# Output projection of layer 1 by row blocks, with a new order of heads and every other weight unit of that mixer split on GpSimd

## The chip, the cores and the metric

The kernel runs on one core of one Trainium2 chip. The metric is the device time of one execution in microseconds (us). The engines are TensorE (PE, with PEld for its weight loads), VectorE (DVE), ScalarE (ACT), GpSimd (POOL) and SyncE (SP), which here issues nearly all DMAs.

## The reference

256 tokens of width 1024 go through two layers and a final RMSNorm, in float32. What the change touches lies in layer 1, between its two feed-forward halves (cut):

```python
u = rmsnorm(h, mix_norm[l])
proj = u @ b_w_q[j]                                  # 6 heads of 128 columns, then 256 for the memory queries
q = partial_rope(proj[..., :MIX_WIDTH]..., cos, sin)
q_mem = proj[..., MIX_WIDTH:]
lam = jnp.exp(jnp.sum(lp[0] * lp[1])) - jnp.exp(jnp.sum(lp[2] * lp[3])) + lam_init
o = differential_attention(q, k_sh, v_sh, lam)       # softmax 1 - lam * softmax 2, causal, times v
y_main = (rmsnorm(o, b_subln[j]) * (1.0 - lam_init)).reshape(b, s, MIX_WIDTH)
y_mem = memory_attention(q_mem, mk, mv)              # 4 heads over 256 memory rows
h = h + jnp.concatenate([y_main, y_mem], axis=-1) @ b_w_out[j]
h = h + 0.5 * swiglu(rmsnorm(h, ffn_post_norm[l]), ffn_post_w1[l], ffn_post_w2[l])
```

## The kernel before, in words

Activations lie transposed: 8 tiles of 128 features by 256 tokens. Every float32 weight comes by DMA into a "raw" tile (1 MB, `rawp`, 4 buffers) and is used in **units** of 128 x 1024 (`hlp`, 5 buffers). A unit is split in `emit_units`: ACT copies it to a reduced type (the high part `wh`, L187), DVE subtracts that from the raw weight (the low part `wl`, L188). Activations are split alike: high part on ACT (L262), low part on DVE (L263 or L268). A product is then three matmuls of 128 x 256 (`mm3`, L339 to L342) or two, of 256 and 512 columns (`mm_wide`, L344 to L348). `next_unit` (L194) hands out unit i and has units up to i+4 split ahead.

The mixer of layer 1 is a hand-written order, the string `ORDER_B` (L18), walked token by token in L903 to L932. With i the head or step: q = query projection of one unit (24 matmuls) and rope (shuffle L678 and product L679 on DVE, L680 and L681 on POOL); A = scores of a head, four maxima on DVE (L826), four exponentials on ACT (L832) and the combination of the two softmaxes on DVE (L834 to L837); T = its transposes on PE (L843) and the copy to SBUF on DVE (L845); P = product with the values on PE (L851 to L853), squares on ACT (L857) and the head's norm on DVE (L280 to L284, L860, L864); D = transposes back (L871) and the split of the result y (L262, L263). For the memory heads m = queries, S = scores (L575, maxima L581), t = transposes (L594) and copy (L596), p = product (L605), N = their norm, O = the way back.

G is a step of the output projection over the first four of its eight column blocks. `Group` (L392) takes four units of 128 output columns each and holds four PSUM tiles; G of step k adds what y[k] gives to each of the four (12 matmuls). After the loop `out_proj` (L488) adds these four blocks to the residual h and computes the other four with a whole unit each (16 matmuls by `mm_wide`). `done_into` (L498) splits each new block of h for the next feed-forward half and adds its square to an accumulator, on POOL for blocks 1 to 6. That half (`ffn_up`, L434) starts with two units of gate columns.

Each engine works through its own instructions in the order of the program; PE in particular doesn't step over a matmul whose operand is late.

Of the kernel before, what the change touches and what calls it, by code (L numbers as in the profile page):

```python
# [42 lines left out]
def decoder_trunk(  # L43
# [155 lines left out]

# [23 lines left out]
    for kp in (2, 3):  # L223
        load_x(2 * kp, 2)
        for o in (0, 1):
            load_w(kp, o, nc.sync)
    zero_b = const.tile([P, P], BF16, name="zero_b")
    V.memset(zero_b, 0.0)
    ps_w = psat.tile([P, 512], F32, tag="at", name="ps_w")
    for i in range(34):  # L230
# [11 lines left out]
    mask_b = const.tile([P, 3 * P], BF16, name="mask_b")  # L242
    V.memset(mask_b[:, P:2 * P], 0.0)
    for b in (0, 2):
        make_causal_mask(nc, mask_b[:, b * P:(b + 1) * P], mask_val=-1e30)
    pos_i = const.tile([P, T], I32, name="pos_i")
    rope_sb = const.tile([P, 2], F32, name="rope_sb")
    lam_sb = const.tile([P, 4 * HD], F32, name="lam_sb")

    def col(base, k):  # L250
        return cols_sb[:, base + k:base + k + 1]
# [140 lines left out]
    class Group:  # L392
        def __init__(self, n):
            self.ws = [next_unit() for _ in range(n)]
            self.ps = [mm_tile() for _ in range(n)]
            self.count = 0

        def run(self, u, ks):
            for w, ps in zip(self.ws, self.ps):
                for i, k in enumerate(ks):  # L400
                    n = self.count + i
                    mm3(ps, at(w, k), u[k], n == 0, n == KD - 1)
            self.count += len(ks)

    def proj_group(u, order=tuple(range(KD))):
        g = Group(2)
        g.run(u, order[:-1])
        g.run(u, order[-1:])
        return g.ps
# [15 lines left out]
    def first_blocks(u):  # L425
        pss = [wide_tile() for _ in range(4)]
        for kp in range(KD // 2):
            w = next_unit()
            for kk in range(2):
                k = 2 * kp + kk  # L430
                for i, ps in enumerate(pss):
                    mm_wide(ps, at(w, kk, slice(i * P, (i + 1) * P)), u[k], k == 0, k == KD - 1)
        return pss

    def ffn_up(u, nrm, after_first=None, rB=None, first=None):
# [49 lines left out]
            if d2 == 0 and after_first is not None:  # L485
                after_first()

    def out_proj(y, done, order, first=None):  # L488
        narrow = 0 if first is None else len(first)
        first = group_wide(y, order) if first is None else first  # L490
        for d in range(KD):
            ps = first[d] if d < len(first) else proj_wide(y, order)
            V.tensor_tensor(out=h[d], in0=ps[:, :T], in1=h[d], op=ALU.add)
            if d >= narrow:
                V.tensor_tensor(out=h[d], in0=ps[:, T:], in1=h[d], op=ALU.add)
            done(d)

    def done_into(nrm, gbase, eng=V):  # L498
# [61 lines left out]
    class MemAttn:  # L560
# [47 lines left out]
        def norm(self):  # L608
            rs = small.tile([P, 2, 4], F32, tag="mrs", name="mrs", bufs=1)
            V.reciprocal(rs, self.sm)  # L610
            on = tmp.tile([P, 2, 4, HD], F32, tag="eT", name="on")
# [16 lines left out]
    St = const.tile([P, T], F32, name="St")  # L628

    def rope_tables():  # L630
        ang = tmp.tile([P, T], F32, tag="t0", name="ang")
        V.tensor_copy(out=ang, in_=pos_i)
        V.tensor_scalar(out=ang, in0=ang, scalar1=rope_sb[:, 0:1], scalar2=None, op0=ALU.mult)
        est = tmp.tile([P, T], F32, tag="sd", name="est", bufs=1)
# [32 lines left out]
    shuf = [i + half if i < half else (i - half if i < ROT else i) for i in range(32)]  # L667

    def rope_scaled(rB):
        cr = tmp.tile([P, T], F32, tag="cr", name="cr", bufs=1)  # L670
        sr = tmp.tile([P, T], F32, tag="sr", name="sr", bufs=1)
# [57 lines left out]
    for j2 in range(3):  # L729
# [21 lines left out]
        step += 1  # L751
        for i in range(2):
            j = 2 * j2 + i
            bg = folded(proj_wide(u), "cr", bufs=1)
# [38 lines left out]
    lt = small.tile([P, 2, HD], F32, tag="lt", name="lt", bufs=1)
    lam4 = lam_sb.rearrange("p (a b d) -> p a b d", a=2, b=2)
    V.tensor_tensor(out=lt, in0=lam4[:, :, 0, :], in1=lam4[:, :, 1, :], op=ALU.mult)
    ls = small.tile([P, 2], F32, tag="ls", name="ls", bufs=1)
    V.tensor_reduce(out=ls, in_=lt, axis=AX.X, op=ALU.add)
# [105 lines left out]
    for tok in ORDER_B:  # L903
        c, i = tok[0], int(tok[1:] or 0)
        if c == "q":
            do_q(i, ready.pop(0) if tok in first else None)
        elif c == "m":
            qm[i] = mem_q(i, ready.pop(0) if tok in first else proj(u))
            if i == 1:
                ma = MemAttn(mkv1, qm, scol, True)  # L910
        elif c == "A":
            stage(i)
        elif c == "T":
            tr(i)
        elif c == "P":
            pv(i)
        elif c == "D":
            out_head(i)
        elif c == "S":
            ma.scores(i)  # L920
        elif c == "t":
            ma.tr(i)
        elif c == "p":
            ma.pv(i)
        elif c == "N":
            ma.norm()
# [117 lines left out]
```

## Time and profile before

| | |
|---|---|
| median of 3 runs | 980.94 us (980.48 to 982.2) |
| profiled execution: its time | 979.39 us |
| profiled execution: span in the trace | 977.6 us |
| PE busy | 961.7 us, 98% |
| DVE / ACT / POOL busy | 760.6 / 594.7 / 42.1 us |
| mixer of layer 1 on PE, first projection to the last output block | 706.07 to 784.51 us |

Busy time is the sum of an engine's instructions; a row of the timeline gives start, duration, engine, source line, operation, output and inputs, and in brackets how long the engine had stood idle before it and what ended that. PEclk is TensorE's granted clock, 1.00 for full speed. Durations of matmuls overlap, so the work of a group on PE is read from start to start.

### The profile page before, as it was taken

Reading aid. Unit: us, or ns where it says so; the run is one execution under the profiler, and the core shown is the slowest. Engines: PE = TensorE matmul, PEld = TensorE weight load, DVE = VectorE, ACT = ScalarE, POOL = GpSimd, SP = SyncE. Lnnn points to the kernel's source line nnn. Section 1 sums busy time; section 2 is a strip of 40 time slices with the busy share of each in tenths; the row PEclk is TensorE's granted clock in tenths of the full one; section 3 lists DMA queues with packets and bytes.
Section 4 is the critical chain, followed back from the end, with each engine's and each line's share of the span. In section 5 each row is a group of like instructions: output and inputs, shape, how many; then the busy total and the mean of one; then the engine's idle time right before and its main releaser. Section 6 shows DMA issues by size and latency. Waiting matters only on the chain.

```text
span 977.6 us, 15066 instructions
## 1 busy us (share of the span) xinstructions
PE 961.7 (98%) x5718; PEld 848.6 (87%) x5718; DVE 760.6 (78%) x1349; ACT 594.7 (61%) x1084; POOL 42.1 (4%) x55
## 2 busy tenths in 40 slices
PE   8999999999999999999999999999997999999997
PEld 7888888888888888888899888888896988888885
DVE  6977877697899987857797887867698688888553
ACT  6876665566556666655664666655558477666452
POOL 2000000001000000000050000000040100000000
PEclk9999999999999999999999999999998999999999
DMA  9866555554555656555556556466542256556441
GB/s 297 287 213 205 163 195 192 185 184 161 167 179 172 216 174 205 171 193 181 192 179 200 187 181 208 163 197 195 181 144 74 78 198 197 192 180 207 154 149 43
DMA packets 168968, 176.92 MB, mean 181 GB/s; under 512 B 3392, under 2 KB 163136, under 8 KB 168896
## 3 DMA queue, kind: packets, MB, share of 16 engines
q1 hardware_dynamic: 168320, 175.39, 55.3%
q8 instruction: 45, 0.74, 0.3%
q10 hardware_dynamic: 576, 0.57, 0.2%
q14 instruction: 27, 0.22, 0.1%
HBM read 174.90 MB, written 1.05 MB: 180 GB/s over the span
## 4 chain that ended last, share of the span: by engine, by line
PE 93%; DVE 4%; ACT 1%; issue 0%; SPq 0%; DMA 0%; POOL 0%; DVEq 0%; ACTq 0%; POOLq 0%
PE ps_mm L348 52%; PE ps_mm L347 27%; PE ps_mm L340 4%; PE ps_mm L341 4%; PE ps_mm L342 4%; DVE wl L188 1%; ACT ed L832 1%; PE ps_mo L605 1%; DVE u L263 1%; PE ps_s L575 0%; DVE nm L826 0%; DMA raw<-pre_w 0%; DVE ed L837 0%; PE ps_t L594 0%; PE ps_n L291 0%
## 5 line engine op out<-in xcount | busy, mean ns | idle before, releaser
L348 PE MATMUL ps_mm<-u,wh 128*128 128x512 f32 x1616 | 564.0, 393 | 0.4 <-DVE u L263 0.2
L188 DVE TENSOR_TENSOR wl<-raw,wh 128x1024 fp32r<-128x1024 f32 (+2 forms) x336 | 404.8, 1206 | 94.4 <-ACT wh L187 84.9
L347 PE MATMUL ps_mm<-u,wl 128*128 128x256 f32 x1616 | 454.8, 282 | 2.8 <-DVE wl L188 2.5
L187 ACT CAST wh<-raw 128x1024 fp32r<-128x1024 f32 (+2 forms) x336 | 345.7, 1032 | 114.2 <-PE ps_mm L348 68.4
L348 PEld LDWEIGHTS ps_mm<-u,wh 128*128 128x128 f32 x1616 | 303.2, 188 | 67.6 <-DVE u L263 1.3
L347 PEld LDWEIGHTS ps_mm<-u,wl 128*128 128x128 f32 x1616 | 306.2, 190 | 4.8 <-DVE wl L188 3.1
L352 ACT COPY half<-ps_mm 128x256 f32<-128x256 f32 x230 | 85.3, 373 | 193.4 <-PE ps_mm L348 193.0
L348 PE MATMUL ps_mm<-g,wh 128*128 128x512 f32 x528 | 183.2, 391 | 0.0
L347 PE MATMUL ps_mm<-g,wl 128*128 128x256 f32 x528 | 147.8, 280 | 0.0
L348 PEld LDWEIGHTS ps_mm<-g,wh 128*128 128x128 f32 x528 | 98.7, 187 | 21.6
L347 PEld LDWEIGHTS ps_mm<-g,wl 128*128 128x128 f32 x528 | 99.8, 189 | 0.0
L353 DVE TENSOR_TENSOR t<-ps_mm,half 128x256 f32<-128x256 f32 x88 | 36.9, 424 | 34.6 <-ACT half L352 34.6
L353 DVE TENSOR_TENSOR up_t<-ps_mm,half 128x256 f32<-128x256 f32 x88 | 37.3, 424 | 29.0 <-ACT half L352 29.0
L462 DVE TENSOR_TENSOR t<-up_t,t 128x256 f32<-128x256 f32 x88 | 37.3, 424 | 2.6
L262 ACT ACTIVATE u<-h,cols_sb 128x256 fp32r<-128x256 f32 x56 | 27.8, 506 | 18.6 <-DVE h L483 12.4
L454 DVE TENSOR_TENSOR t<-t,rB 128x256 f32<-128x256 f32 x88 | 36.8, 424 | 2.4
L267 ACT CAST g<-t 128x256 fp32r<-128x256 f32 x88 | 35.4, 407 | 3.9 <-DVE t L462 3.5
L455 ACT ACTIVATE t<-t 128x256 f32<-128x256 f32 x88 | 36.1, 418 | 1.6 <-DVE t L454 1.0
L268 DVE TENSOR_TENSOR g<-t,g 128x256 fp32r<-128x256 f32 x88 | 36.6, 420 | 0.4
L341 PE MATMUL ps_mm<-wl,g 128*128 128x512 f32 x88 | 34.3, 389 | 0.0
L340 PE MATMUL ps_mm<-wh,g 128*128 128x512 f32 x88 | 34.2, 389 | 0.0
L342 PE MATMUL ps_mm<-wh,g 128*128 128x512 f32 x88 | 34.2, 389 | 0.0
(231 smaller groups left out, 912.5 us busy)
## 6 DMA issues: line engine op xcount, KB each, us to landing
raw<-post_w SPq DMA_DIRECT2D x62, 1024.0 KB, 5.1
raw<-pre_w SPq DMA_DIRECT2D x58, 1024.0 KB, 5.1
raw<-a_w_in SPq DMA_DIRECT2D x10, 1024.0 KB, 5.2
raw<-pre_w SPq DMA_DIRECT2D x8, 768.0 KB, 4.4
raw<-kv_w SPq DMA_DIRECT2D x6, 1024.0 KB, 5.1
raw<-w_kv SPq DMA_DIRECT2D x4, 1024.0 KB, 5.4
raw<-a_w_out SPq DMA_DIRECT2D x4, 1024.0 KB, 5.1
raw<-b_w_q SPq DMA_DIRECT2D x4, 1024.0 KB, 5.2
```

What stands on the lines that cost most here:

```text
L187: S.copy(out=hv, in_=src)
L188: V.tensor_tensor(out=lv, in0=src, in1=hv.bitcast(F32), op=ALU.subtract)
L268: V.tensor_tensor(out=dst[1], in0=src, in1=dst[0].bitcast(F32), op=ALU.subtract)
L340: TE.matmul(ps, a[0], b[0], start=start, stop=False)
L341: TE.matmul(ps, a[0], b[1], start=False, stop=False)
L342: TE.matmul(ps, a[1], b[0], start=False, stop=stop)
L347: TE.matmul(ps[:, :T], a[1], b[0], start=start, stop=False, skip_group_check=True)
L348: TE.matmul(ps, a[0], b[2], start=False, stop=stop, skip_group_check=True)
L352: S.copy(out=half, in_=ps[:, T:])
L353: V.tensor_tensor(out=out, in0=ps[:, :T], in1=half, op=ALU.add)
L454: V.tensor_tensor(out=t, in0=t, in1=rB, op=ALU.mult)
L462: V.tensor_tensor(out=ts_[i], in0=up_t, in1=ts_[i], op=ALU.mult)
```

## The change: what it does

- **Order.** `ORDER_B` is written anew: four of the six D come later, the memory steps earlier, and G0 and G1 stand before the last head's transposes. G6 and G7 leave the string.
- **Row blocks.** `Rows` takes the place of `Group` and `out_proj`: a unit of b_w_out is now 128 rows of it (one k) by all 1024 columns, and G of step k is 24 matmuls, three for each of eight output blocks, which lie in four PSUM banks. `finish` does k = 6 and 7 block by block, adds each block to h and hands it on. The squares of h are summed on DVE alone.
- **Low parts on GpSimd.** `on_pool` names ten units, every other one from the second of b_w_q on: four of b_w_q, four of b_w_out, two of the next feed-forward half. Their subtraction goes to POOL.
- **Prefetch.** Six buffers of `hlp` and i+5 in place of five and i+4.
- **Next half.** `ffn_up` starts with four units at once, k outermost (`four_blocks`).
- Room for the sixth buffer comes from small tiles folded into others (mask, positions, rope tables, results of the memory heads).

```diff
+ORDER_B = ("q0 q1 q2 A0 A1 q3 q4 T0 A2 P0 q5 T1 A3 P1 m0 D0 A4 T2 D1 S0 m1 P2 A5 T3 t0 T4 P4 t1 S1 G0 "
+           "D2 G1 T5 t2 P3 p0 t3 P5 G2 D3 p1 p2 p3 D5 N D4 G3 O G4 G5").split()
...
-    hlp = ctx.enter_context(tc.tile_pool(name="hlp", bufs=5))
+    hlp = ctx.enter_context(tc.tile_pool(name="hlp", bufs=6))
...
+    on_pool = range(len(units) + 1, len(units) + 20, 2)
...
-    for j2 in range(4):
-        units.extend(plan_cols(b_w_out, j2 * 256))
+    for k in range(0, KD, 2):
+        ri = add_raw(b_w_out, k, 2, 0, D)
+        units.extend([(D, [(ri, o, 1, 0, 0)]) for o in (0, 1)])
...
-                V.tensor_tensor(out=lv, in0=src, in1=hv.bitcast(F32), op=ALU.subtract)
+                (G if i in on_pool else V).tensor_tensor(out=lv, in0=src, in1=hv.bitcast(F32), op=ALU.subtract)
...
-        emit_units(i + 4)
+        emit_units(i + 5)
...
+    class Rows:
...
+        def __init__(self):
+            self.banks = [wide_tile() for _ in range(KD // 2)]
...
+        def step(self, w, b, k, d):
...
+            ps, a = self.block(d), at(w, 0, slice(d * P, (d + 1) * P))
+            TE.matmul(ps, a[0], b[0], start=(k == 0 and d % 2 == 0), stop=False, skip_group_check=True)
+            TE.matmul(ps, a[0], b[1], start=False, stop=False, skip_group_check=True)
+            TE.matmul(ps, a[1], b[0], start=False, stop=(k == KD - 1), skip_group_check=True)
...
+        def run(self, y, k):
+            w = next_unit()
+            for d in range(KD):
+                self.step(w, y[k], k, d)
...
+        def finish(self, y, done):
+            ws = {k: next_unit() for k in (KD - 2, KD - 1)}
+            for d in range(KD):
+                for k, w in ws.items():
+                    self.step(w, y[k], k, d)
+                V.tensor_tensor(out=h[d], in0=self.block(d), in1=h[d], op=ALU.add)
+                done(d)
...
+    def four_blocks(u):
+        ws = [next_unit() for _ in range(4)]
+        pss = [wide_tile() for _ in range(4)]
+        for k in range(KD):
+            for w, ps in zip(ws, pss):
+                mm_wide(ps, at(w, k), u[k], k == 0, k == KD - 1)
...
-    out_proj(y, done_into(nrm, C_POST + 8, G), tuple(range(KD)), grp.ps)
+    st["grp"].finish(y, done_into(nrm, C_POST + 8))
...
-    gs, rB = ffn_up(nrm.u, nrm, after_first=to_natural)
+    gs, rB = ffn_up(nrm.u, nrm, after_first=to_natural, first=four_blocks)
```

On PE, before: from the last head's scores (A5, `kT`) and S0 to the first step G0 (L340). L851 to L853 are a P, L843 a T, L871 a D, L575 an S, L594 a t; the first P below is P2, the second P3.

```order
4348 L822 MATMUL ps_s<-kT_5364,q_7896 128x128 x6
4349 L575 MATMUL ps_s<-mkT_5603,qm 128x256 x4
4350 L851 MATMUL ps_o<-vN_5370,aT 128x128
...
4353 L843 MATMUL ps_t<-ident,ed 128x128 x3
4354 L871 MATMUL ps_t<-ident,o_7985 128x128 x2
4355 L851 MATMUL ps_o<-vN_5370,aT 128x128
...
4358 L843 MATMUL ps_t<-ident,ed 128x128 x3
4359 L575 MATMUL ps_s<-mkT_5631,qm 128x256 x4
4360 L871 MATMUL ps_t<-ident,o_8073 128x128 x2
4361 L851 MATMUL ps_o<-vN_5370,aT 128x128
```

On PE, now: the same place, with line numbers moved (L850 is A, L871 a T, L624 a t, L879 to L881 a P, L605 an S, L409 to L411 a G, of 24 matmuls; L899 a D). The P is P4, and y_8021 is y[0].

```order
4354 L850 MATMUL ps_s<-kT_5367,q_7923 128x128 x6
4355 L871 MATMUL ps_t<-ident,ed 128x128 x3
4356 L624 MATMUL ps_t<-ident,me_8072 128x128 x4
4357 L871 MATMUL ps_t<-ident,ed 128x128 x3
4358 L879 MATMUL ps_o<-vN_5373,aT 128x128
...
4361 L624 MATMUL ps_t<-ident,me_8078 128x128 x4
4362 L605 MATMUL ps_s<-mkT_5634,qm 128x256 x4
4363 L409 MATMUL ps_mm<-y_8021,wh 128x256
```

Before, two P, a T, an S and two D of 0.2 to 1 us each stood between the last scores and the next long run of matmuls; now P4, t1 and S1 lead over to G0, and P3 and P5 stand behind G1.

On POOL, now, from the layer's shared keys on: L191 is the subtraction of a unit, L713 and L714 are the two rope operations of a query. Before, the twelve rope operations stood alone, with six accumulations of h's squares behind them.

```order
27 L191 TENSOR_TENSOR wl<-raw,wh 128x1024 x3
28 L713 TENSOR_TENSOR k_s<-k_s,St 128x256
29 L714 TENSOR_TENSOR q_7664<-q_7664,k_s 128x256
30 L713 TENSOR_TENSOR k_s<-k_s,St 128x256
31 L714 TENSOR_TENSOR q_7670<-q_7670,k_s 128x256
32 L191 TENSOR_TENSOR wl<-raw,wh 128x1024
...
37 L191 TENSOR_TENSOR wl<-raw,wh 128x1024
...
42 L191 TENSOR_TENSOR wl<-raw,wh 128x1024 x5
```

The subtractions of units 1, 3 and 5 (counted from the first of b_w_q) stand ahead of the first query's rope, that of 7 behind the second's, that of 9 behind the fourth's, those of 11 to 19 behind the last's.

## Rows read from the trace of the kernel before

**Rows 1.** The page: busy time by engine, and the chain that ended last.

```profile
PE 961.7 (98%) x5718; PEld 848.6 (87%) x5718; DVE 760.6 (78%) x1349; ACT 594.7 (61%) x1084; POOL 42.1 (4%) x55
...
PE 93%; DVE 4%; ACT 1%; issue 0%; SPq 0%; DMA 0%; POOL 0%; DVEq 0%; ACTq 0%; POOLq 0%
```

**Rows 2.** Busy time by windows: stretch, PE, PEld, DVE, ACT, POOL, granted clock, DMA.

```profile
706.00:742.50 36.50, 36.50 (x322) 33.16 (x320) 33.37 (x97) 23.55 (x68) 11.57 (x12) 1.00 0.46 146
742.50:747.40 4.90, 0.09 (x2) 0.07 (x1) 4.87 (x18) 3.71 (x16) 0.00 (x0) 0.96 0.00 2
747.40:750.00 2.60, 2.60 (x11) 2.27 (x13) 1.24 (x4) 2.60 (x12) 0.00 (x0) 0.50 0.00 0
750.00:753.40 3.40, 3.40 (x17) 2.58 (x16) 2.42 (x11) 1.86 (x10) 0.00 (x0) 0.50 0.00 0
753.40:756.00 2.60, 2.30 (x18) 2.08 (x17) 2.34 (x12) 2.60 (x14) 0.00 (x0) 0.91 0.00 0
```

**Rows 3.** What PE waited for, 706 to 792 us: total, times, longest.

```profile
PE ps_o L851 <- DVE hrs L284: 0.3, 1, 0.3
```

**Rows 4.** Timeline of PE in the mixer and behind it.

```profile
706.07 0.28 PE L340 MATMUL ps_mm<-u,wh 128*128 128x256 f32 x1
...
741.85 0.49 PE L843 MATMUL ps_t<-ident,ed 128*128 128x128 f32 x3
742.17 0.38 PE L871 MATMUL ps_t<-ident,o 128*128 128x128 f32 x2
747.36 0.77 PE L851 MATMUL ps_o<-vN,aT 128*128 128x128 f32 x2 [4.81 <-DVE ri L834]
...
760.21 0.60 PE L594 MATMUL ps_t<-ident,me 128*128 128x128 f32 x4
760.65 1.00 PE L605 MATMUL ps_mo<-mv,eT 128*128 128x64 f32 x8
...
784.51 0.28 PE L347 MATMUL ps_mm<-u,wl 128*128 128x256 f32 x1
...
788.31 0.40 PE L348 MATMUL ps_mm<-u,wh 128*128 128x512 f32 x1
788.54 0.28 PE L347 MATMUL ps_mm<-u,wl 128*128 128x256 f32 x1
788.66 0.40 PE L348 MATMUL ps_mm<-u,wh 128*128 128x512 f32 x1
...
791.90 0.61 PE L291 MATMUL ps_n<-acc,ones 128*128 128x128 f32 x4
```

**Rows 5.** DVE in the mixer: weight splits by group (706 to 750.2 us), then timeline.

```profile
L188 DVE TENSOR_TENSOR wl<-raw,wh 128x1024 fp32r<-128x1024 f32 x10 | 12.7, 1267 | 0.0
...
746.67 0.55 DVE L845 COPY aT<-ps_t 128x384 f32<-128x384 f32 x1
749.66 0.56 DVE L845 COPY aT<-ps_t 128x384 f32<-128x384 f32 x1 [1.32 <-PE ps_t L843]
750.20 0.48 DVE L263 SCALAR_TENSOR_TENSOR y<-ps_t,gsub,y 128x256 fp32r<-128x256 f32 x1
754.94 0.69 DVE L596 COPY eT<-ps_t 128x512 f32<-128x512 f32 x1
```

**Rows 6.** Timelines of DVE and of POOL, where the two work side by side.

```profile
713.31 1.73 DVE L188 TENSOR_TENSOR wl<-raw,wh 128x1024 fp32r<-128x1024 f32 x1
718.53 1.14 DVE L826 TENSOR_REDUCE nm<-ps_s 128x1 f32<-128x128 f32 x4
...
727.11 0.69 DVE L835 SCALAR_TENSOR_TENSOR ri<-ri,nlam,sm 128x2 f32<-128x2 f32 x1
...
713.91 1.72 POOL L680 TENSOR_TENSOR k_s<-k_s,St 128x256 f32<-128x256 f32 x1
718.66 0.73 POOL L681 TENSOR_TENSOR q<-q,k_s 128x256 f32<-128x256 f32 x1
727.04 0.74 POOL L681 TENSOR_TENSOR q<-q,k_s 128x256 f32<-128x256 f32 x1
```

More of the change, by code (lines that the diff above doesn't have):

```diff
@@ L226, in decoder_trunk @@
             load_w(kp, o, nc.sync)
-    zero_b = const.tile([P, P], BF16, name="zero_b")
+    mask_b = const.tile([P, 3 * P], BF16, name="mask_b")
+    zero_b = mask_b[:, P:2 * P]
     V.memset(zero_b, 0.0)
@@ L241, in decoder_trunk @@
     make_identity(nc, ident)
-    mask_b = const.tile([P, 3 * P], BF16, name="mask_b")
-    V.memset(mask_b[:, P:2 * P], 0.0)
     for b in (0, 2):
         make_causal_mask(nc, mask_b[:, b * P:(b + 1) * P], mask_val=-1e30)
-    pos_i = const.tile([P, T], I32, name="pos_i")
     rope_sb = const.tile([P, 2], F32, name="rope_sb")
-    lam_sb = const.tile([P, 4 * HD], F32, name="lam_sb")
+    early = memp.tile([P, D], F32, tag="vg", name="early")
+    lam_sb = early[:, 0:4 * HD]
+    pos_i = early[:, T:2 * T].bitcast(I32)
+    lt = early[:, 2 * T:2 * T + 2 * HD].rearrange("p (a d) -> p a d", d=HD)
+    ls = const.tile([P, 2], F32, name="ls")
     def col(base, k):
@@ L390, in proj, with block @@
         return ps
[L392 to L403, printed above, removed]
-    def proj_group(u, order=tuple(range(KD))):
[L406 to L409, printed above, removed]
+    class Rows:
+        def __init__(self):
+            self.banks = [wide_tile() for _ in range(KD // 2)]
+        def block(self, d):
+            return self.banks[d // 2][:, (d % 2) * T:(d % 2 + 1) * T]
+        def step(self, w, b, k, d):
[14 more added lines that the diff above has]
+                done(d)
+    def proj_group(u, order=tuple(range(KD))):
+        ws = [next_unit() for _ in range(2)]
+        pss = [mm_tile() for _ in range(2)]
+        for ks in (order[:-1], order[-1:]):
+            for w, ps in zip(ws, pss):
+                for k in ks:
+                    mm3(ps, at(w, k), u[k], k == order[0], k == order[-1])
+        return pss
     def toks(u, th):
@@ L432, in first_blocks @@
                     mm_wide(ps, at(w, kk, slice(i * P, (i + 1) * P)), u[k], k == 0, k == KD - 1)
+        return pss
+    def four_blocks(u):
+        ws = [next_unit() for _ in range(4)]
+        pss = [wide_tile() for _ in range(4)]
+        for k in range(KD):
+            for w, ps in zip(ws, pss):
+                mm_wide(ps, at(w, k), u[k], k == 0, k == KD - 1)
         return pss
@@ L486, in ffn_down, with out_proj @@
                 after_first()
-    def out_proj(y, done, order, first=None):
-        narrow = 0 if first is None else len(first)
-        first = group_wide(y, order) if first is None else first
+    def out_proj(y, done, order):
+        first = group_wide(y, order)
         for d in range(KD):
@@ L493, in out_proj @@
             V.tensor_tensor(out=h[d], in0=ps[:, :T], in1=h[d], op=ALU.add)
-            if d >= narrow:
-                V.tensor_tensor(out=h[d], in0=ps[:, T:], in1=h[d], op=ALU.add)
+            V.tensor_tensor(out=h[d], in0=ps[:, T:], in1=h[d], op=ALU.add)
             done(d)
@@ L610, in norm @@
             V.reciprocal(rs, self.sm)
-            on = tmp.tile([P, 2, 4, HD], F32, tag="eT", name="on")
+            on = big.tile([P, 2, T], F32, tag="g21", name="on").rearrange("p a (h d) -> p a h d", d=HD)
             V.tensor_tensor(out=on, in0=self.po, in1=rs.unsqueeze(3).broadcast_to([P, 2, 4, HD]), op=ALU.mult)
@@ L630, in rope_tables @@
     def rope_tables():
+        lam4 = lam_sb.rearrange("p (a b d) -> p a b d", a=2, b=2)
+        V.tensor_tensor(out=lt, in0=lam4[:, :, 0, :], in1=lam4[:, :, 1, :], op=ALU.mult)
+        V.tensor_reduce(out=ls, in_=lt, axis=AX.X, op=ALU.add)
         ang = tmp.tile([P, T], F32, tag="t0", name="ang")
@@ L633, in rope_tables @@
         V.tensor_scalar(out=ang, in0=ang, scalar1=rope_sb[:, 0:1], scalar2=None, op0=ALU.mult)
-        est = tmp.tile([P, T], F32, tag="sd", name="est", bufs=1)
+        est = tmp.tile([P, T], F32, tag="q", name="est", bufs=3)
         rr = tmp.tile([P, 3, T], F32, tag="ed", name="rr", bufs=3)
@@ L669, in rope_scaled @@
     def rope_scaled(rB):
-        cr = tmp.tile([P, T], F32, tag="cr", name="cr", bufs=1)
-        sr = tmp.tile([P, T], F32, tag="sr", name="sr", bufs=1)
+        tab = tmp.tile([P, 3, T], F32, tag="ed", name="tab", bufs=3)
+        cr, sr = tab[:, 0, :], tab[:, 1, :]
         V.tensor_tensor(out=cr, in0=Ct, in1=rB, op=ALU.mult)
@@ L753, in decoder_trunk @@
             j = 2 * j2 + i
-            bg = folded(proj_wide(u), "cr", bufs=1)
+            bg = folded(proj_wide(u), f"t{i}")
             V.tensor_tensor(out=cvs[i], in0=bg, in1=cvs[i], op=ALU.mult)
@@ L791, in decoder_trunk @@
     u = nrm.u
[L793 to L797, printed above, removed]
     gsub = small.tile([P, 1], F32, tag="gsub", name="gsub", bufs=1)
@@ L908, in decoder_trunk @@
             qm[i] = mem_q(i, ready.pop(0) if tok in first else proj(u))
-            if i == 1:
+            if i == 0:
                 ma = MemAttn(mkv1, qm, scol, True)
@@ L930, in decoder_trunk @@
             if st["grp"] is None:
-                st["grp"] = Group(4)
-            st["grp"].run(y, (i,))
-    grp = st["grp"]
+                st["grp"] = Rows()
+            st["grp"].run(y, i)
     nrm = Norm(False)
-    out_proj(y, done_into(nrm, C_POST + 8, G), tuple(range(KD)), grp.ps)
+    st["grp"].finish(y, done_into(nrm, C_POST + 8))
     gB = memp.tile([P, D], F32, tag="vg", name="gB")
@@ L952, in to_natural @@
                 S.copy(out=hn[th][:, q4 * 512:(q4 + 1) * 512], in_=pt)
-    gs, rB = ffn_up(nrm.u, nrm, after_first=to_natural)
+    gs, rB = ffn_up(nrm.u, nrm, after_first=to_natural, first=four_blocks)
     rc = fin["rc"]
-    sums = [const.tile([P, 4], F32, name=f"sums{th}") for th in range(2)]
-    rest = [const.tile([P, 1], F32, name=f"rest{th}") for th in range(2)]
-    rf = [const.tile([P, 1], F32, name=f"rf{th}") for th in range(2)]
+    row = const.tile([P, 2, 6], F32, name="row")
+    sums = [row[:, th, 0:4] for th in range(2)]
+    rest = [row[:, th, 4:5] for th in range(2)]
+    rf = [row[:, th, 5:6] for th in range(2)]
     def finish(th, d4, ps):
```

4 lines of the change are left out of this document (1 added, 3 removed).

## The prediction

> **What bounds the kernel now.** I read the page first, then windows along the span, then PE's waits and its timeline where it waits, then DVE's and POOL's timelines beside it. The page says that PE is busy 98% of the span and carries 93% of the chain that ended last [rows 1]. So only time in which PE stands still, runs at the lower clock, or does work that can be left out is to be had. The changed mixer holds one such place. Up to 742.5 us PE is full, with DVE busy 33.4 of 36.5 us; then PE has 0.09 us of work in 4.9 while DVE is busy throughout [rows 2]. The timeline names the piece: 4.81 us of idleness before the matmuls of P3 [rows 4]. The view puts it down to the reciprocal L834, but the operand of that P is a copy aT, which DVE starts only at 746.67 [rows 5], though its transposes were through at about 742.2 [rows 4]. So DVE is behind with its queue, and PE, which goes by its order, waits.
>
> The stop costs a second time. After it the granted clock stands at 0.50, the lower of the two levels (1.2 instead of 2.4 GHz), from 747.4 to 753.4 us, and at 0.91 on average up to 756 [rows 2]: half of 6.0 us and 9% of 2.6 are 3.2 us. Another 0.3 us goes at the last head's P [rows 3]. A last loss lies behind the mixer: from 784.51 to 791.90 us, 7.39 us, PE does two units of gate columns [rows 4]. Each has 8 matmuls of 512 columns at 0.23 us and 8 of 256 at 0.12, start to start, 2.8 us, so 5.6 is work and 1.8 is waiting for the last blocks of h. All in all 4.8 + 3.2 + 0.3 + 1.8 = 10.1 us is what the change could reach.
>
> **The change part by part.**
>
> *PE's list.* The mixer takes 784.51 - 706.07 = 78.44 us [rows 4]; without 4.8, 0.3 and 3.2 it is 70.1 us of work. The output projection grows a little: four of its eight units took 16 matmuls of 256 and 512 columns (2.8 us) and now take 24 of 256 (24 x 0.12 = 2.9), with a few more changes of operand; I add 0.3 and have 70.4. Before P3, the fourth P in the old list, PE needed 36.5 us [rows 2]. The fourth P of the new one, P4, has the same ahead of it and one T more (0.32, from 741.85 to 742.17), one D (two transposes where a T has three, 0.2) and a t (0.44, from 760.21 to 760.65) [rows 4], 37.5 us in all. Behind it 70.4 - 37.5 = 32.9 us of work are left, most of it in the steps G, 24 matmuls each where 12 stood. Those are long enough to hide the memory heads, the last head and the norms.
>
> *DVE up to the operand of that P.* P4 uses the copy of T4, the fifth aT. Before, the fifth copy starts at 749.66, 43.6 us into the mixer, after 1.32 us in which DVE waited for PE at its low clock [rows 5]. In the new order five units fewer are split by DVE in this stretch (five instead of the group's ten [rows 5]). Without the long one of [rows 6] the other nine of the group took (12.7 - 1.73) / 9 = 1.2 us each, so that is 6.0 us less. Ahead of the copy now stand two splits of y (0.48 each) and a copy of a memory head (0.69) [rows 5], 1.65 us more. So the copy starts at 43.6 - 1.3 - 6.0 + 1.65 = 37.9 us, plus what the subtractions on POOL cost DVE. Four of them run in this stretch, those of units 5, 7, 9 and 11.
>
> *What such a subtraction costs DVE.* No row shows one. Its own length is bounded by POOL's 128x256 operations, 0.74 us [rows 6]: four times that, 2.95 us, as the upper end; scaled as DVE's go from 0.48 for 256 columns to 1.2 for 1024 [rows 5], 1.85 us. I take 2.5, being nearer the former as each row of POOL's work is of the same kind. What it does to DVE shows where the ropes run: DVE's subtraction at 713.31 took 1.73 us instead of 1.2, POOL's operation at 713.91 took 1.72 instead of 0.74, and the tiny L835 at 727.11 took 0.69 beside a POOL operation of 0.74; but the maxima at 718.53, which read PSUM, took 1.14 for all four beside POOL's 718.66, whole as it was (0.73) [rows 6]. So a DVE instruction that reads only SBUF stands still until POOL's is through, and one that reads PSUM doesn't. The cost of one is then between 0 (DVE is at its maxima, copies from PSUM or idle) and 2.5 us (a blocked instruction is next at once). DVE's work here is mixed: the four maxima of a head alone are 1.1 us. I take **1.0 us**, under the middle, because units 5 and 7 run while DVE has some slack before the first scores. Four of them make 4.0, so the copy starts at 41.9, and P4 0.7 us later as at the old P3 (746.67 to 747.36 [rows 4, 5]): 42.6 us. With 0 it is 38.6, with 2.5 it is 48.6.
>
> *The rule against this.* The row of L835 shows nearly the whole length of a POOL operation lost. The Trainium skill, "SBUF — State Buffer", section "Who interferes with whom", says that a DVE instruction with two inputs in SBUF contends with a GpSimd one that reads SBUF, that the pair of ports is held for a whole instruction, and that the other side fully blocks. The trace agrees (0.69 of 0.74). By that rule taken strictly a subtraction would cost some 2 us, and the sum would come out as in the third rival. "GPSIMD Engine Reference", section "Performance versus the Vector engine", gives 4497 ns for 2048 columns of such an operation, from which 2.2 us for one subtraction is an estimate; with it the third rival would be shorter by about an eighth.
>
> *Where the waits go.* PE would reach P4 at 37.5 and goes on at 42.6, so some 5 us of waiting stay. In the old order it was one stop, since five tokens stood between A0 and T0 and two between T0 and P0. Now it is three and one: T0, P0, P1 wait a little each, and P4 for the rest. With no stop of several us I take the clock as staying at its upper level, and the 3.2 us as gained.
>
> *Behind P4.* 32.9 us without a stop: y of each head is due long before its G, except the last (D5, two tokens of 3 us ahead of G5). The mixer then takes 42.6 + 32.9 = 75.5 us, 2.9 less.
>
> *The end of the projection.* The last two k go block by block, 48 matmuls or 5.8 us, so the blocks of h are ready early and the next half starts with four units, 11 us of PE work that needs the last block only in its last 1.4 us. DVE has per block an addition, a split and a square, each 0.5 us at most by the split of y [rows 5], so 12 us for eight under 16.8 us of PE. The 1.8 us of waiting goes. Moving the six squares from POOL to DVE is hidden there too; without this cover it would cost up to 6 x 0.5 us.
>
> *Nothing, I think:* the DMAs of b_w_out carry the same bytes, and the DMA share up to 742.5 is 0.46 [rows 2], so the later release of a raw tile by POOL has room; if not, a unit late by a DMA of 5 us would be seen. The merged tiles, the earlier reading of lambda and the folded tables cost DVE and ACT nothing that PE waits for. The first subtraction on POOL could hold up DVE's last block of h and with it the last step of the first query, by 1 us; that would be one of the waits already counted.
>
> Sum: -2.9 - 1.8 = **-4.7 us**. The profiled execution of 979.39 us becomes 974.7; the median lies 1.55 above it, and 980.94 becomes **976.2 us**.
>
> **The rivals.** Two per mille, 2 us, is about what a measurement of this kernel can tell from no change; in that scale:
>
> *The subtractions are hidden (0.24).* If most of POOL's time falls on DVE's waits and its PSUM work, P4 comes at 38.6 or earlier. The mixer is 78.44 - 38.6 - 32.9 = 6.9 us shorter, with the 1.8 it is -8.7: 972.2 us. For it: DVE is idle 3 of its 36.5 us already with ten subtractions [rows 2], and would be idle more with five. Against: L835 and the stretched 1.73.
>
> *The waits fall in one piece again (0.18).* PE keeps 5 us of waiting before P4, as DVE's lag adds up there, and the clock drops for 6 us as it did after the old stop. The 3.2 us are then not gained: -1.5, 979.4 us. For it: the old order kept PE full for 36.5 us with the same lag growing unseen.
>
> *GpSimd holds DVE for most of each subtraction (0.19).* The place is the same, P4 behind the fifth copy. At 2.0 us each the copy starts at 45.9 and P4 at 46.6: the mixer is 79.5 us, the stop at P4 is long and costs the 3.2 us of clock again, 82.7. With the 1.8 that is +2.5: 983.4 us; at 2.5 us each 985.4. It decides from about 1.35 us a subtraction if the clock falls, from 2.2 if it doesn't. For it: DVE has a blocked instruction (a subtraction, L835, L837, the norms) every us or so. Against: the first two subtractions meet slack.
>
> *It does nothing (0.03).* DVE isn't the limit but ACT's exponentials are, and P4 waits as before: within 1 us of 980.9. ACT is busy 23.6 of 36.5 us [rows 2], which speaks against it.
>
> **How the numbers follow.** My forecast has 0.36; with 1.0 +- 0.4 us a subtraction it spans 974.6 to 977.8. The range takes in the first and second rivals and the third up to 2.1 us a subtraction: 971.0 to 984.0. Faster by over 2 us: my forecast, the first rival (0.60). Within 2 us: most of the second, the last (0.20). Slower: the third (0.20 with what I have not thought of).
>
> **What would show it.** Right: in the new trace DVE has five L191 up to the fifth aT copy and POOL subtractions of about 2.5 us; DVE instructions on SBUF beside them are stretched; PE's waits are several of under 2 us, at T0, P0, P1 and P4, 5 us in sum; the granted clock is 1.00 through the mixer; its length is 75.5; no wait is left ahead of the L291 matmuls. Wrong: a single wait of over 4 us before P4, or a clock of 0.5 behind it, or subtractions of over 3 us, or a wait of G for a weight unit or for y, which I have priced at nothing.

## The result, and the profile after

The changed kernel takes **994.83 us** (median, 993.73 to 995.77) beside 981.01 us of the kernel before on the same chip: a ratio of 1.0146, 95% interval 1.0133 to 1.0158. It is slower by 13.8 us where 4.7 less were forecast, and lies outside the range.

The page of the changed kernel, the two lines that answer to [rows 1]: PE is busy for 3.9 us more in a span of 992.3 us in place of 977.6, and POOL for 18 us more.

```profile
PE 965.6 (97%) x5750; PEld 850.7 (86%) x5750; DVE 762.1 (77%) x1340; ACT 592.6 (60%) x1083; POOL 60.3 (6%) x59
...
PE 92%; DVE 4%; ACT 1%; issue 1%; SPq 0%; DMA 0%; POOL 0%; DVEq 0%; ACTq 0%; POOLq 0%
```

PE's timeline: the mixer's first row, its two long stops (P0 and P4), the last stop, and the first matmul of 512 columns behind the mixer, in this text the first wide one:

```profile
709.95 0.28 PE L345 MATMUL ps_mm<-u,wh 128*128 128x256 f32 x1
...
736.64 0.77 PE L879 MATMUL ps_o<-vN,aT 128*128 128x128 f32 x2 [3.66 <-DVE aT L873]
...
764.41 0.76 PE L879 MATMUL ps_o<-vN,aT 128*128 128x128 f32 x2 [6.12 <-DVE hrs L888]
...
797.93 0.39 PE L409 MATMUL ps_mm<-ym,wh 128*128 128x256 f32 x1 [1.21 <-DVE h L423]
...
800.07 0.40 PE L353 MATMUL ps_mm<-u,wh 128*128 128x512 f32 x1
```

In the kernel before the first wide one is this:

```profile
784.63 0.40 PE L348 MATMUL ps_mm<-u,wh 128*128 128x512 f32 x1
```

Against the kernel before (706.07 to 784.63) the mixer begins 3.9 us later and is 90.12 us long instead of 78.56, 11.6 more; what follows takes 992.3 - 800.07 = 192.2 instead of 193.0. That is the whole 14.7 us of the spans. Inside the mixer, by windows (PE, PEld, DVE, ACT, POOL, clock, DMA), the answer to [rows 2]:

```profile
709.95:735.00 25.05, 20.17 (x170) 17.93 (x168) 22.78 (x46) 12.07 (x29) 14.68 (x11) 0.98 0.36 126
735.00:742.00 7.00, 5.36 (x29) 5.39 (x30) 5.17 (x18) 3.28 (x14) 2.33 (x2) 0.57 0.46 150
736.64:742.00 5.36, 5.36 (x29) 5.36 (x30) 3.53 (x13) 3.28 (x14) 1.57 (x1) 0.59 0.50 172
742.00:758.30 16.30, 15.38 (x134) 12.89 (x132) 14.17 (x41) 10.76 (x36) 3.86 (x3) 1.00 0.20 66
758.30:764.40 6.10, 0.00 (x0) 0.02 (x1) 5.03 (x14) 3.36 (x13) 2.34 (x1) 0.76 0.10 25
764.40:768.50 4.10, 4.09 (x18) 3.27 (x18) 2.56 (x9) 2.21 (x10) 0.00 (x0) 0.52 0.66 225
```

The third line is the part of the second from P0 on. The granted clock falls during each of the two stops and stays at its lower level for some us behind it. That costs time only where PE works: 41% of the 5.36 us from P0 on and 48% of the 4.1 us from P4 on are 4.2 us. PE's stops in the mixer sum to 14.6 us. 90.1 - 14.6 - 4.2 = 71.3 us is work, 0.9 more than forecast (70.4). So the loss is nearly all waiting and clock, and the cause shows where DVE and POOL stand side by side. First POOL's subtractions of units 5, 7, 9, 11 and 13, with the rope operation behind that of unit 7; then the DVE rows that begin beside them, with a free row of L865 (751.15) and the copy that P4 waits for (763.72):

```profile
712.32 2.39 POOL L191 TENSOR_TENSOR wl<-raw,wh 128x1024 fp32r<-128x1024 f32 x1 [2.88 <-ACT wh L190]
721.71 2.36 POOL L191 TENSOR_TENSOR wl<-raw,wh 128x1024 fp32r<-128x1024 f32 x1
724.03 0.74 POOL L713 TENSOR_TENSOR k_s<-k_s,St 128x256 f32<-128x256 f32 x1
732.45 2.35 POOL L191 TENSOR_TENSOR wl<-raw,wh 128x1024 fp32r<-128x1024 f32 x1
744.53 2.45 POOL L191 TENSOR_TENSOR wl<-raw,wh 128x1024 fp32r<-128x1024 f32 x1
760.17 2.34 POOL L191 TENSOR_TENSOR wl<-raw,wh 128x1024 fp32r<-128x1024 f32 x1 [13.18 <-ACT wh L190]
```

```profile
712.42 2.58 DVE L514 TENSOR_TENSOR ft<-ft,rBh 128x256 f32<-128x256 f32 x1
...
722.04 2.05 DVE L587 TENSOR_SCALAR scol<-rc 128x2 f32<-128x2 f32 x1
724.01 0.41 DVE L712 TENSOR_TENSOR q<-ps_mm,Ct 128x256 f32<-128x256 f32 x1
...
732.55 2.80 DVE L865 SCALAR_TENSOR_TENSOR ed<-ed,ri 128x128 f32<-128x128 f32 x2
...
743.96 3.31 DVE L865 SCALAR_TENSOR_TENSOR ed<-ed,ri 128x128 f32<-128x128 f32 x2
...
751.15 0.75 DVE L865 SCALAR_TENSOR_TENSOR ed<-ed,ri 128x128 f32<-128x128 f32 x2
...
760.55 1.97 DVE L287 TENSOR_TENSOR hrs<-rsca 128x2 f32<-128x2 f32 x1
...
763.72 0.55 DVE L873 COPY aT<-ps_t 128x384 f32<-128x384 f32 x1
```

Beside every one of the five a DVE instruction stands that begins within 0.4 us of it, or before it, and ends with it or at most 0.6 us later. L514 loses 2.2 us against the 0.4 of such a row, L587 1.9 and L287 1.8 against the 0.16 of such rows elsewhere, L865 2.05 and (less some 0.5 that a rope takes) 2.06 against its 0.75 at 751.15. That is 10.0 us. The last lies right ahead of the fifth aT (763.72), for which P4 waits. The stop of 1.2 us near the end is a sixth case: the subtraction of unit 19 holds a split of u, 0.48 us elsewhere, and the addition to h that PE waits for stands behind it on DVE.

```profile
794.53 2.40 POOL L191 TENSOR_TENSOR wl<-raw,wh 128x1024 fp32r<-128x1024 f32 x1 [3.79 <-ACT wh L190]
795.20 2.01 DVE L268 SCALAR_TENSOR_TENSOR u<-h,cols_sb,u 128x256 fp32r<-128x256 f32 x1 [0.58 <-ACT u L267]
```

### The profile page after: what moved, and what is told of

It reads as the page before. It is cut to its first block, busy times and chain, and to the rows that moved or that the text cites. A ratio compares the mean times of both kernels' runs of the same rounds, so it can differ in the third digit from the quotient of the medians.

```text
span 992.3 us, 15123 instructions
## 1 busy us (share of the span) xinstructions
PE 965.6 (97%) x5750; PEld 850.7 (86%) x5750; DVE 762.1 (77%) x1340; ACT 592.6 (60%) x1083; POOL 60.3 (6%) x59
## 4 chain that ended last, share of the span: by engine, by line
PE 92%; DVE 4%; ACT 1%; issue 1%; SPq 0%; DMA 0%; POOL 0%; DVEq 0%; ACTq 0%; POOLq 0%
PE ps_mm L353 51%; PE ps_mm L352 27%; PE ps_mm L346 3%; PE ps_mm L345 3%; PE ps_mm L347 3%; PE ps_mm L409 1%; PE ps_mm L411 1%; PE ps_mm L410 1%; PE ps_mo L635 1%; DVE ed L865 1%; DVE wl L191 1%; ACT ed L860 1%; DMA h<-xT 0%; PE ps_s L605 0%; PE ps_t L624 0%
## 5 line engine op out<-in xcount | busy, mean ns | idle before, releaser
L191 DVE TENSOR_TENSOR wl<-raw,wh 128x1024 fp32r<-128x1024 f32 (+2 forms) x326 | 393.0, 1207 | 96.8 <-ACT wh L190 87.8
L191 POOL TENSOR_TENSOR wl<-raw,wh 128x1024 fp32r<-128x1024 f32 x10 | 23.9, 2385 | 245.8 <-ACT wh L190 245.8
L345 PE MATMUL ps_mm<-wh,g 128*128 128x512 f32 x88 | 34.3, 390 | 0.0
```

The source lines that it names most:

```text
L191: (G if i in on_pool else V).tensor_tensor(out=lv, in0=src, in1=hv.bitcast(F32), op=ALU.subtract)
L345: TE.matmul(ps, a[0], b[0], start=start, stop=False)
```

## The experiments

**Theory H**: GpSimd holds DVE for most of each subtraction. **Theory O**: the new order makes the waits. A later question (**pace**) is the 3.9 us ahead of the mixer. In all runs the mixer is measured from its first matmul to the first wide one behind it, as above. A **pair** is one matmul of 256 and one of 512 columns, and its pace is the time from the start of one pair to that of the next.

### All low parts on DVE, GpSimd added to the kernel before, and the old order

e1:

```diff
-    on_pool = range(len(units) + 1, len(units) + 20, 2)
+    on_pool = ()
```

> The changed kernel with all low parts back on DVE (on_pool empty); new order, row blocks, prefetch and four_blocks stay. Theory H (a subtraction on GpSimd holds DVE for about its whole 2.4 us where DVE would need 1.2): the holds of units 5, 7, 9, 11 and 13 read from the changed kernel's trace (2.2, 2.3, 2.05, 2.4, 1.8 us, 10.8 in all) go and 5 x 1.2 us come back, so the mixer is about 5 us shorter, more if the clock stays up at one of its two stops: 980 to 990 us. Theory O (the new order makes the waits whatever engine subtracts): no more than 2 us off the changed kernel's 994.8.

983.53 us, ratio 1.0034 (1.0022 to 1.0046); the mixer is 78.17 us. 11 of the 14 us are GpSimd's. The new order does split the old single stop: PE waits 0.4, 0.35, 0.85, 1.75 and 2.6 us. But the last of these waits, at P4, is still followed by a stretch at half clock, which costs 1.7 us:

```profile
755.53 0.46 PE L879 MATMUL ps_o<-vN,aT 128*128 128x128 f32 x2 [2.61 <-DVE hrs L289]
```

```profile
755.53:757.00 1.47, 1.47 (x10) 1.28 (x10) 1.22 (x3) 1.42 (x7) 0.00 (x0) 0.79 0.06 17
757.00:759.00 2.00, 2.00 (x9) 1.19 (x8) 1.75 (x8) 0.78 (x4) 0.00 (x0) 0.50 0.52 146
759.00:760.00 1.00, 1.00 (x6) 0.85 (x5) 1.00 (x4) 0.00 (x0) 0.00 (x0) 0.60 1.09 388
```

e2, the kernel before with `on_pool` and the changed subtraction line alone:

> The kernel before with the same ten subtractions on GpSimd and nothing else. Theory H: some 1 us of DVE time lost per subtraction in the mixer, so the stop before P3 grows by 4 to 8 us: 985 to 989 us. Theory O: GpSimd takes 6 us of work off DVE ahead of the stop, so 980 us or less.

995.15 us, 1.0149 (1.0134 to 1.0164), mixer 87.08 us. DVE was given ten subtractions less and got later. More than expected: the mixer alone is 8.5 us longer, and behind it, where later subtractions run beside DVE's splits of u, PE waits 3.2 us for u.

e3, the changed kernel with the old order:

```diff
+ORDER_B = ("q0 q1 q2 A0 q3 A1 q4 A2 q5 T0 A3 m0 P0 T1 A4 m1 P1 T2 A5 S0 P2 T3 D0 P3 T4 S1 D1 P4 T5 t0 D2 "
+           "P5 G0 p0 t1 G1 D3 t2 p1 G2 D4 t3 p2 G3 p3 N D5 G4 O G5").split()
```

> The changed kernel with the old order of tokens (without G6 and G7, which finish does); row blocks, GpSimd, prefetch stay. Theory H: the holds stay, so slower than before by 4 to 8 us less the 1.8 us won behind the mixer: 983 to 988 us. Theory O: the waits made by the new order go, so 979 us or less.

991.44 us, 1.0116 (1.0099 to 1.0132), mixer 84.48: more than either theory had. With GpSimd at work, the new order is worse than the old by 3 us.

e4, the same with `on_pool = ()`:

> Row blocks, prefetch and four_blocks alone: old order, all low parts on DVE. Both theories: the stop before P3 and its clock stay as before, the 1.8 us behind the mixer are won: 979 us. Against e1 it shows what the new order alone does: theory H has e1 within 3 us of it, theory O has e1 10 us or more above it.

983.55 us, 1.0029 (1.0014 to 1.0045), mixer 78.21. Equal to e1: without GpSimd the orders give the same. Theory O falls. But both are 3 us over the kernel before, where e4 was to be 2 under it, although their mixers are no longer than its 78.56.

### The hold by itself

e7 (five buffers, four ahead, all low parts on DVE; GpSimd repeats ten subtractions for nobody):

```diff
+                if i in on_pool:
+                    G.tensor_tensor(out=spare_t.rearrange("p (k c) -> p k c", c=w)[:, kd:kd + kn], in0=src, in1=hv.bitcast(F32), op=ALU.subtract)
```

> All low parts on DVE, five buffers and four ahead as before, new order and row blocks; besides, GpSimd makes the same ten subtractions a second time into a tile that nobody reads. DVE is relieved of nothing and only the side-by-side remains. Theory H: the holds of 1.8 to 2.4 us come on top, 5 of them in the stretch that bounds: 992 to 1000 us. A theory by which a late result of GpSimd is what PE waits for: 984 us, since nobody waits for these.

993.17 us, 1.0138 (1.0118 to 1.0158); mixer 87.81, 9.6 over that of e5 (e1 with units split four ahead, told of below). e8, which has five buffers as well, has 78.20, so the buffers don't matter. Nobody waits for these results, so it is the subtractions' running that costs, not their lateness. Not all of it is DVE's being held: a query's rope stands behind an extra subtraction in POOL's own queue, and one stop of PE is put down to it (0.4 us at the same place in e5):

```profile
PE ps_s L853 <- POOL q L717: 2.7, 1, 2.7
```

How DVE is held shows in its row beside POOL's of 711.13 (2.40 us): a split, elsewhere 1.2 us long, takes 2.2 more:

```profile
711.18 3.44 DVE L192 TENSOR_TENSOR wl<-raw,wh 128x1024 fp32r<-128x1024 f32 x1
```

It works the other way too: where DVE begins first, POOL's subtraction takes 3.44 us in place of 2.4. One row of each engine:

```profile
705.43 1.22 DVE L192 TENSOR_TENSOR wl<-raw,wh 128x1024 fp32r<-128x1024 f32 x1 [1.60 <-ACT wh L191]
705.48 3.44 POOL L194 TENSOR_TENSOR spare_t<-raw,wh 128x1024 f32<-128x1024 f32 x1 [202.01 <-ACT wh L191]
```

e8 (three fills of that tile instead of the subtraction):

> As e7, but in place of each extra subtraction GpSimd fills the tile three times after the same ACT copy: it writes SBUF and reads nothing. Theory H with the read ports as the place: no DVE instruction is stretched beside it and the time is that of e5, 980 to 984 us. If GpSimd held DVE whatever it does: as e7.

983.97 us, 1.0050 (1.0032 to 1.0067). It says nothing: the fills, which wait for nobody, ran at 6 to 43 us. e9 makes them wait:

```diff
+                    S.copy(out=spare_t[:, 0:1], in_=src[:, 0, 0:1])
+                    for _ in range(3):
+                        G.memset(spare_t, 0.0)
```

> e8 again, since its fills ran at the start of the kernel, where nothing held them back: here ACT first writes one column of the extra tile behind each of the ten high parts, so the three fills (0.95 us each, 2.9 us) run where e7 has its subtractions. Theory H with the read side as the place: DVE isn't stretched and the time is e5's and e8's, 983 to 986 us with ten more ACT instructions of 0.2 us. If GpSimd's writes hold DVE as well: as e7, 993 us.

985.99 us, 1.0054 (1.0037 to 1.0071); mixer 80.88, 2.6 over e5's. What shows of the cause is the added ACT copy: it waits for POOL's earlier fills, 2.21 us at one place, a head's exponentials and DVE's queue stand behind it, and PE's wait at P1 is 3.6 us instead of 1.8.

```profile
737.27 0.19 ACT L194 COPY spare_t<-raw 128x1 f32<-128x1 f32 x1 [2.21 <-POOL spare_t L196]
```

Beside the fills DVE isn't stretched. POOL's fills and a DVE split in their middle:

```profile
722.37 2.96 POOL L196 MEMSET spare_t<- 128x1024 f32 x3
```

```profile
724.24 1.21 DVE L192 TENSOR_TENSOR wl<-raw,wh 128x1024 fp32r<-128x1024 f32 x1
```

So in these runs a GpSimd instruction that reads SBUF holds DVE, and one that only writes doesn't. e11 cuts each subtraction of the changed kernel in four:

```diff
+                    for q0 in range(0, kn * w, 256):
...
+                            G.tensor_tensor(out=lv[:, 0, qs_], in0=src[:, 0, qs_], in1=hv[:, 0, qs_].bitcast(F32), op=ALU.subtract)
```

> The changed kernel with each subtraction on GpSimd cut in four instructions of 256 columns, 0.74 us each by the ropes. Theory H with the lock held for one instruction: DVE waits 0.7 us at most at a time and gets its turn between the quarters, so the stretched instructions of 2 us and more go; GpSimd's results come later. 986 to 991 us, between e1 and the changed kernel. If a lock lasted for the whole series, or the loss were one of total GpSimd time, 994 us or more.

987.48 us, 1.0080 (1.0067 to 1.0094); mixer 82.09. POOL takes longer in all (3.01 us for four) and DVE loses less: L865, 2.80 us in the changed kernel, is 1.65 here at the same place.

```profile
731.64 1.65 DVE L874 SCALAR_TENSOR_TENSOR ed<-ed,ri 128x128 f32<-128x128 f32 x2
```

The hold is for one instruction: DVE gets its turn behind a quarter. Some 7 of the 11 us come back, 4 stay. e6 has GpSimd subtract units 13 to 19 alone:

```diff
+    on_pool = range(len(units) + 13, len(units) + 20, 2)
```

> The changed kernel with only units 13, 15, 17 and 19 on GpSimd, which run after the heads' scores. Theory H: cost goes with what DVE has to do beside them; in the changed kernel those of 13, 15 and 19 held DVE for 1.8, 1.0 and 1.5 us, that of 13 right before the copies that P4 waits for. So up to 2 us above e1 (983.5), 983 to 986 us. If only the length of the stretch counted, no difference.

987.77 us, 1.0085 (1.0068 to 1.0102), more than expected; mixer 82.31, 4.1 over e1. The wait at P4 grows from 2.6 to 4.4 us and that for h to 1.2: even the late ones run beside DVE work that PE waits for.

### The 3 us ahead of the mixer

Groups of wide matmuls in the second layer's first feed-forward half, by form: the kernel before (530 to 700 us), then the changed one (532 to 703). The code there is the same.

```profile
L348 PE MATMUL ps_mm<-u,wh 128*128 128x512 f32 x333 | 115.5, 391 | 0.0
L347 PE MATMUL ps_mm<-u,wl 128*128 128x256 f32 x332 | 93.0, 280 | 0.0
L348 PE MATMUL ps_mm<-g,wh 128*128 128x512 f32 x159 | 55.2, 391 | 0.0
```

```profile
L353 PE MATMUL ps_mm<-u,wh 128*128 128x512 f32 x329 | 116.3, 399 | 0.0
L352 PE MATMUL ps_mm<-u,wl 128*128 128x256 f32 x328 | 92.2, 281 | 0.0
L353 PE MATMUL ps_mm<-g,wh 128*128 128x512 f32 x156 | 55.2, 399 | 0.0
```

From start to start a pair takes 347 ns before and 353 after, for some 500 pairs: 3.3 us, with the granted clock at 1.00 in both. The traces of the five kernels at 347 ns (the kernel before, e2, e14, e15, e17) reach the mixer at 706.1 to 707.9 us, those of the others at 709.5 to 712.5.

e5, `emit_units(i + 4)` in e1: 

> e1 with units split four ahead as before in place of five (six buffers stay). In e1, e3, e4 and the changed kernel a pair of wide matmuls takes 353 ns instead of 347 from the second layer's first feed-forward half up to the mixer (some 500 pairs, 3.4 us). Theory prefetch: the deeper prefetch brings this, so it goes here, and the time is 3 us under e1: 980. Theory layout or chance of phase: it stays, 983 us.

983.12 us, 1.0036 (1.0021 to 1.0051): pairs stay at 353 ns, so the prefetch isn't the cause. Nor is the number of buffers: e7, e8 and e9, with five, have 353 too.

e10, the small matmul on `ones` of `ffn_up` repeated at the next two pairs: 

> e1 with the small matmul on ones that stands behind the second layer's first two feed-forward units repeated behind the next two pairs. In the kernel before, wide pairs go from 353 to 347 ns behind the first of them; in e1 they stay at 353. Theory phase (the slow pace is a state of PE's pipeline that such a matmul can end): pairs go to 347 ns and the time falls by 3 us to 980. Otherwise 983.5.

984.19 us, 1.0043 (1.0026 to 1.0061), 353 ns. e14, the kernel before without that matmul: 

> The kernel before without its one small matmul on ones behind the second layer's first two feed-forward units, behind which its wide pairs go from 353 to 347 ns. If that matmul ends the slow pace there: pairs stay at 353 ns up to the mixer, 500 x 6.6 ns, 3.3 us slower, 984 us. If the pace has another cause: 980.9 us as before.

981.53 us, 1.0017 (1.0004 to 1.0031), 347 ns. That matmul neither makes nor ends the pace; my reading of its place in the trace was wrong.

e15, the kernel before with `Rows`, its plan of units, `finish` and `four_blocks`: 

> The kernel before with row blocks and four_blocks alone: old order (without G6 and G7), all low parts on DVE, five buffers, four ahead, and the small tiles where they were. Differs from e4 by the tiles' places and the prefetch only. If those bring the 353 ns pace, it is 347 here and the time is 1.8 us under before, 979; if the row blocks bring it, 353 and 982 to 983.

979.30 us, 0.9991 (0.9981 to 1.0001), 347 ns. Row blocks don't bring it. What is left between e15 and e4 is the moving of small tiles, with the few instructions that moved along (lambda is read earlier). e17 and e18 test one form of it, in the kernel before and in the changed one:

```diff
+    pad = const.tile([P, 8], F32, name="pad")
```

> The kernel before with the same unused tile of 32 bytes and nothing else: its weight and activation tiles now begin at odd multiples of 32 bytes. Theory place: wide pairs of the second layer's first feed-forward half take 353 ns and the time rises by 3.3 us to 983. If the place doesn't matter: 980.

> The changed kernel with the same unused tile: its tiles now begin at multiples of 64 bytes. Theory place: 347 ns there and 3.3 us less than the changed kernel, 991 us, the rest of the loss (11 us) being GpSimd's. If the place doesn't matter: 994.5.

980.77 us, 1.0001 (0.9993 to 1.0010), still 347 ns; and 996.67 us, 1.0167 (1.0149 to 1.0184), still 353. A shift by 32 bytes isn't it. What brings the pace stays open.

### Can the waits be covered at all?

The old order had more small work between its last scores and G0 than the count ahead of the prediction: four P, three T, three D, two S and a t. The new one left P4, t1 and S1 in front of G0, and P4 was where PE waited longest. e12, on e10:

```diff
+ORDER_B = ("q0 q1 q2 A0 A1 q3 q4 T0 A2 q5 P0 T1 A3 m0 P1 D0 A4 T2 S0 D1 m1 P2 A5 T3 t0 T4 t1 S1 G0 P4 "
+           "D2 G1 T5 t2 P3 p0 t3 P5 G2 D3 p1 p2 p3 D5 N D4 G3 O G4 G5").split()
```

> e10 with some tokens moved so that long matmul runs stand before the products P that waited in e1 (0.85 us at P0, 1.75 at P1, 2.6 at P4): q5 ahead of P0, m0 ahead of P1, G0 ahead of P4. If DVE is late by a fixed time there, the waits shrink from 6.0 to about 1 us and the half clock behind P4 goes: the mixer is 5 to 7 us shorter, 974 to 976 us, faster than both kernels. If DVE's queue just moves the wait to the next token, 980 us as e10.

982.94 us, 1.0031 (1.0019 to 1.0044): the waits at P0, P1 and P4 are gone, one of 3.4 us stands at D1 instead, and the time is not the 974 to 976 hoped for. e13 moves D1 behind m1: 

> e12 with D1 behind m1: its only long stop in e12 (3.4 us, then 1.2 us of half clock) is D1 before m1, waiting for the norm of P1. If m1's 2.9 us cover it, the mixer falls from 77.4 to 73 us and the time by 4 us to 979. Besides, small matmuls of five other shapes stand behind the pairs 2 to 6 of the second layer's first feed-forward half: if one of them ends the 353 ns pace, up to 3.3 us more go, 976, and the trace shows which; if none does, the pace doesn't depend on such a matmul.

979.69 us, 1.0002 (0.9991 to 1.0013): the mixer is 74.00 us, but the pace stays, and no small matmul of any shape ended it for long. e16 takes e13's order with the old small matmul and the unused tile: 

> e13 without its mixed small matmuls (only the one of the kernel before) and with an unused tile of 32 bytes in the first pool, which moves all later tiles by 32 bytes. In the kernels whose wide pairs took 347 ns the weight and activation tiles begin at multiples of 64 bytes in their partition (wh at 83008), in those with 353 ns at odd multiples of 32 (wh at 80608). Theory place: the pace is 347 ns now and the mixer stays at e13's 74.0 us, together 976 us, faster than both kernels. If the place doesn't matter: 979.7 as e13.

979.22 us, 0.9988 (0.9978 to 0.9998). The pace is 353 ns here too, so 3.3 us of the mixer's 4.6 are given back ahead of it. In the mixer (712.46 to 786.42 us) these are all of PE's waits, and then its windows, the clock in the third column from the end:

```profile
PE ps_t L900 <- DVE o L893: 0.9, 2, 0.4
PE ps_s L851 <- POOL q L715: 0.4, 1, 0.4
PE ps_t L872 <- DVE ed L866: 0.3, 1, 0.3
```

```profile
712.46:740.00 27.54, 26.76 (x232) 24.45 (x231) 25.93 (x67) 15.86 (x43) 12.43 (x12) 1.00 0.44 151
740.00:765.00 25.00, 24.04 (x194) 20.98 (x192) 21.42 (x76) 20.91 (x75) 0.00 (x0) 1.00 0.27 85
765.00:786.42 21.42, 21.42 (x183) 21.17 (x181) 15.31 (x40) 9.78 (x23) 0.00 (x0) 1.00 0.43 146
```

1.6 us of waiting and full clock throughout, so 72.4 us of work: the order could cover DVE's lateness, with every subtraction on DVE. e16 is the one kernel here whose interval lies wholly under the kernel before, by a little. That order in e15, where the pace is 347 ns, was not tried.

## Why the prediction was wrong

- **What bounded the kernel** was right: DVE's queue up to the fifth aT sets P4. The sum without GpSimd's cost holds: 37.9 us, with the subtractions put back on DVE (four or five of 1.2 us: DVE makes nine ahead of that copy in e1, five in the changed kernel) and 0.7 to P4, is 43.4 to 44.6; e1 has P4 at 755.53 - 711.29 = 44.2. PE's work in the mixer, 70.4 us in the forecast, is 71.3 here and 70.5 to 72.4 in e1 and e16, up to 2 us more.
- **The step that failed** is "I take **1.0 us**", the cost of a subtraction to DVE, "because units 5 and 7 run while DVE has some slack". Read from the five rows it is 2.0 us (1.8 to 2.2), units 5 and 7 included, so that each loses 0.8 more than it saves. And five count, not four: that of unit 13 runs ahead of the copy too. The length, 2.5 us, was right (2.34 to 2.45). A value under the middle of two bounds stood for a mechanism whose rows [rows 6] spoke for the upper one: the next instruction that touches only SBUF stops, however small, and in all five cases DVE came to one within 0.4 us.
- **The third rival** had the mechanism and the 2.0 us, but 983.4: it counted four subtractions and one stop. P4 came at 764.41 - 709.95 = 54.5 us instead of 46.6, and with a fifth subtraction it would still be 48.6. What I left out shows beside e1, in DVE's windows from the mixer's first matmul to the fifth copy (the changed kernel, then e1):

```profile
709.95:763.72 53.77, 40.92 (x330) 36.21 (x328) 46.52 (x115) 28.80 (x89) 23.21 (x17) 0.92 0.29 99
```

```profile
711.29:754.84 43.55, 38.24 (x330) 34.15 (x328) 39.77 (x118) 28.74 (x89) 11.54 (x12) 1.00 0.35 120
```

  The copy comes 10.2 us later. DVE is busy for 6.7 us more: it has 4.5 less of weight subtractions and 11.2 more of the rest, 10.0 of them the five holds. And it stands idle for 3.5 us more, waiting for PE (1.7 us for query projections, 0.3 in e1) and for ACT. That fits a held DVE that makes PE and ACT late and then waits for them, though no run shows this part by itself. I had added one lateness at one place.
- **The clock**: "I take the clock as staying at its upper level" failed too. There were two stops of over 3 us, and half clock behind them cost 4.2 us. It failed even without GpSimd, where the wait at P4 is 2.6 us and half clock costs 1.7 (e1). With waits of at most 0.45 us the clock does stay, as e16 shows.
- **Behind the mixer** 0.7 us were won by the marks above. Six matmuls of the mixer, 0.7 us, run behind the first wide one and so stand in what follows it, which makes 1.5 of the 1.8 forecast: right. But the stop of 1.2 us for h, at the end of the mixer, takes most of it back; I had priced the later subtractions at nothing.
- **Not foreseen**: 3.3 us in a stretch that the change doesn't touch. I had priced the merged tiles and the earlier reading of lambda at nothing; whether they are the cause is open.
- **The rule** of the Trainium skill ("SBUF — State Buffer", section "Who interferes with whom") is what the forecast should have gone by. The runs agree with it in three points: a write-only GpSimd instruction doesn't contend (e9), the hold is for a whole instruction (e11), and a DVE instruction with one input in PSUM isn't touched (L712 at 724.01, 0.41 us beside the rope of 724.03). I had named it and then set its price by a guess under it.

## What to carry to other kernels

Before moving work from DVE to GpSimd, look at what DVE does meanwhile. Here each GpSimd subtraction from SBUF cost DVE 1.8 to 2.2 of its 2.4 us, where DVE would have needed 1.2 itself. By the rows it would cost less beside DVE work that reads PSUM, or beside an idle DVE; no run here arranged that. Cutting it into short instructions helped (e11), but leaving it on DVE was better still (e1). Where PE waits for a late DVE queue, put a long run of matmuls that is already fed ahead of the waiting one, follow the wait to where it goes next, and move that too.

## What the runs showed of the hardware that I had not expected

A DVE instruction on 128x2 elements (L587, one input), 0.16 us by itself, took 2.05 us beside a GpSimd instruction on another tile. And PE ran the same pairs of matmuls at 353 or 347 ns at the same granted clock, for 180 us on end, for a reason that stays open: neither the prefetch, nor the buffers, nor the row blocks, nor a shift of all tiles by 32 bytes.
